# A fused mixer and expert kernel: the third down products moved to the down bank, one expert later

## The chip, the cores and the metric

One core of a Trainium2 chip runs the whole kernel in one launch. The metric is device time in microseconds; before the change the median of three runs is 716.4 us (715.74 to 717.3).

## The reference

256 tokens of 1024 channels pass through two hybrid layers (attention over selected keys, a compressed and windowed attention, a short convolution, a pooling mixer) and a norm, then through a second block: a state-space and attention mixer, a layer norm, and a mixture of 16 experts, all in float32. The change lies in the experts alone:

```python
weights = g_val[:, None] * e_val
expert_id = g_idx[:, None] * EXPERTS_PER_GROUP + e_idx
combine = jnp.sum(jax.nn.one_hot(expert_id, N_EXPERTS) * weights[..., None], axis=1)
for e in range(N_EXPERTS):
    act = jax.nn.silu(hf @ w_gate[e]) * (hf @ w_up[e])
    out = out + combine[:, e:e + 1] * (act @ w_down[e])
```

Two experts are chosen for a token, so an expert has 32 tokens on average, and the numbers are known only at run time. A layer norm of the residual and `out` ends the kernel.

## The kernel before, in words

**Blocks.** `experts` (L1941) walks over the 16 experts in four quarters of four; `e` is the expert, `j = e % 4` its place and `q = e // 4` its quarter. For a quarter, `gather_all` multiplies the normed tokens by one-hots (`picks`, on VectorE) and so brings the quarter's tokens into `xg`: 64 places for each expert, and 32 more. `gate_up` (L1730) computes gate and up for blocks of 32 tokens: the first block always, into the PSUM bank `gu`; the second under a branch for more than 32 tokens and the third under one for more than 64, into banks of the tag `s`. Where a block isn't computed, a one-column matmul (`none`, L1726) stands in for it. In this data the experts 0, 2, 4, 6, 8, 10 and 12 have more than 32 tokens, and 4 and 8 have more than 64.

**From gate and up to the output.** `activate` (L1765) reads `gu` on ScalarE and VectorE (L1773, L1774), applies SiLU and the product, and writes `sg`; it then does the same for the second and third block under branches. `turn` (L1791) transposes `sg` on TensorE and copies it to `aT` (two buffers); it is called as `mid`, between the sixth and the seventh of the eight weight tiles of the *next* expert's first block. `down` (L1806) multiplies `aT` by the down weights into the bank `dn`, for up to 64 tokens, and `take` (L1813) copies or adds `dn` into the rows `y[0]` of the expert. `third` (L1832) is the down product of the tokens 64 to 95, under a branch, with a `none` in its place otherwise, and `take_third` (L1841) adds it into `y2`, also under a branch. After every second expert `split_all` (L1859) multiplies the rows of two experts by their routing weights and splits them in a high and a low part (L1856 on ScalarE, L1857 on VectorE), and `scatter_all` (L1682) adds them to the output banks `acc` by matmuls with the turned one-hots `oT`. `spread` (L1628) makes `oT`: it turns the one-hots on TensorE into `dn` in two lots, and ScalarE copies each (L1637).

**Order.** The engines run their programs in the order written; `manual_schedule` keeps it. In the turn of expert `e` it is, for TensorE: the first block of `e` with `turn(e - 1)` inside, the other blocks, a scatter or a spread where due, `down(e - 1)`, `third(e - 1)`. For ScalarE and VectorE: the copy of `turn`, `activate(e)`, `take(e - 1)`, `take_third(e - 1)`, then splits, or the next quarter's `picks` (VectorE, `j == 2`) ahead of the splits. The spread of the first quarter is made in expert 0, that of the others in their third expert (`j == 2`). Expert 15 has an order of its own (L1973 to L1980).

**Weights.** Each expert has three loads of 2 MB, (gate, up) in two and down in one, which SyncE's queue fetches in a fixed order into ten ring buffers (`fill`, L275; the issue is L292). A load is issued when `give_back` (L302) has returned a buffer: those of gate and up after the expert's blocks, that of down after `third`.

A 32-column float32 matmul over 512 columns appears as two records, so the first block (16 matmuls) is 32 records, 24 of them ahead of the turn and 8 behind it.

Of the kernel before, what the change touches and what calls it, by code (L numbers as in the profile page):

```python
# [246 lines left out]
class Net:  # L247
# [1479 lines left out]

        self.nc.tensor.matmul(b[:, 0:1], self.zero, w.bitcast(BF16)[:, 1:2], start=True, stop=True)

    def gate_up(self, e, mid=None):  # L1730

        j, tc = e % 4, self.tc
        ws, rs = zip(*[self.load() for _ in range(2)])
        ws = [a.rearrange("p (k n) -> p k n", k=4) for a in ws]

        def w(k):
            return ws[k // 4][:, k % 4, :]

        def x(s):
            return lambda k: self.S["xg"][:, k, s:s + 32]  # L1740
        banks = self.gus = [self.gu]

        def before():
            if mid:
                mid()
            banks.extend(self.mbank("s") for _ in range(2))

        def none(i):
            for a in ws[2 - i:]:
                self.none(banks[i], a[:, 0, 0:1])  # L1750
        if e + 1 < N_EXP:
            self.count(e + 1)
        self.product32(banks[0], w, KT, x(64 * j), before)
        with tc.If(self.n[e] > 32) as more:
            self.product32(banks[1], w, KT, x(64 * j + 32))
            with tc.If(self.n[e] > 64) as much:
                self.product32(banks[2], w, KT, x(256 + 32 * j))
            with much.Else():
                none(2)
        with more.Else():  # L1760
            none(1)
            none(2)
        self.give_back(*rs)
# [67 lines left out]

    def third(self, e, aT, wd):  # L1832

        b = self.gu
        with self.tc.If(self.n[e] > 64) as more:
            self.product32(b, lambda k: wd[:, k, :], 4, lambda k: aT[:, k, 64:96])
        with more.Else():
            self.none(b, wd[:, 0, 0:1])
        return b
# [101 lines left out]
    def experts(self):  # L1941
        nc, m = self.nc, self.mw
        self.acc = [[self.ps.tile([P, HALF], F32, name=f"acc{t}{h}") for h in range(2)] for t in range(NT)]
        self.gu, self.dn = (self.ps.tile([P, HALF], F32, name=n) for n in ("gu", "dn"))
        self.clear(self.gu)
        self.clear(self.dn)
        for a in self.acc:
            for b in a:
                self.open(b)
        self.sg = m.tile([P, HALF], F32, name="sg")  # L1950
        nc.gpsimd.memset(self.sg, 0.0)
        S = self.S = {}
        self.wq = {}
        NQ = N_EXP // 4

        def gather_all():
            S["xg"] = m.tile([P, KT, 384], F32, name="xg")
            for k in range(KT):
                self.gather(self.oh, S["xg"], k)
                if k == KT - 1:  # L1960
                    self.wq[len(self.wq)] = self.weights(len(self.wq), self.oh)
        gather_all()
        self.residual()
        self.n, self.na = {}, {}
        self.count(0)
        aT = oT = None
        wd = lambda w: w.rearrange("p (k n) -> p k n", k=4)
        E = mybir.EngineType
        nq = naq = None
        for e in range(N_EXP):  # L1970
            q, j = divmod(e, 4)
            more, last = q + 1 < NQ, e == N_EXP - 1
            if last:  # L1973
                aT = self.turn(e - 1)
                self.scatter_all(oT[:, 0, :])
                w, r = self.load()
                self.down(e - 1, aT, wd(w))
                self.take(e - 1)
                self.split_all(slice(0, 64), self.wq[q][:, 1:2])
                self.gate_up(e)  # L1980
            else:
                def mid():
                    nonlocal aT
                    aT = self.turn(e - 1)
                self.gate_up(e, mid if e else None)
            if j == 0 and q:
                c = self.cnt[0:1, 16 + q:17 + q]
                nq = nc.values_load(c, engines=(E.PE,), min_val=0, max_val=T)
                naq = nc.values_load(c, engines=(E.Activation, E.DVE), min_val=0, max_val=T)
            if j == 1 and q:  # L1990
                self.scatter_all(oT[:, 1, :])
            if j == 2 and q:
                with self.tc.If(nq > 64) as much:
                    self.scatter_all(oT[:, 2, :])
                with much.Else():
                    for h in range(2):
                        for y in self.y[1:]:
                            self.nc.tensor.matmul(self.acc[1][h][:, 0:1], self.zero,
                                                  y.bitcast(BF16)[:, h * D + 1:h * D + 2], start=False, stop=False)
                oT = self.spread(self.oh)  # L2000
            if e == 0:
                oT = self.spread(self.oh)
            if j == 3 and more:
                self.scatter_all(oT[:, 0, :])
            if e and not last:
                w, r = self.load()
                self.down(e - 1, aT, wd(w))
            self.activate(e)
            if e and not last:
                self.take(e - 1)  # L2010
                b = self.third(e - 1, aT, wd(w))
                self.give_back(r)
                self.take_third(e - 1, b, self.na[e - 1])
            if j == 1 and q:
                with self.tc.If(naq > 64):
                    self.split_third(q - 1, self.y[1:])
            if j == 2:
                if more:
                    self.oh = self.picks(q + 1)
                self.split_all(slice(0, P), self.wq[q][:, 0:1])  # L2020
            if j == 0 and q:
                self.split_all(slice(0, P), self.wq[q - 1][:, 1:2])
            if j == 3 and more:
                gather_all()
        self.tc.mark_branch_hint_location("further", "LikelyTaken")
        for _ in range(WARM[3]):
            self.clear(self.dn)
        a0, aT = aT, self.turn(N_EXP - 1)
        i = self.free.pop()
        self.last = self.rings[i].tile([P, 4096], F32, name=f"wchunk{i}")  # L2030
        for i in range(2):
            self.row(4 + i, self.last[:, i * D:(i + 1) * D], eng=nc.sync)
        free = list(self.free)[:4]
        left = [(N_EXP - 2, a0, wd(w))]
        w, r = self.load()
        left.append((N_EXP - 1, aT, wd(w)))
        for _ in range(WARM[4]):
            self.clear(self.dn)
        self.down(N_EXP - 1, aT, wd(w))
        self.take(N_EXP - 1, True)  # L2040
        self.further(free, left, oT)
        self.scatter_all(oT[:, 1, :], last=True)
# [65 lines left out]
```

## Time and profile before

| | |
|---|---|
| median of three runs | 716.4 us |
| the profiled execution's own time | 718.6 us |
| its span, from first to last instruction | 716.8 us |
| TensorE matmul busy | 634.8 us (89%) |
| VectorE busy | 445.2 us (62%) |
| ScalarE busy | 315.1 us (44%) |
| mean granted TensorE clock | 0.947 |
| HBM traffic | 227 GB/s over the span |
| expert stage, first block of expert 0 to first block of expert 15 | 443.1 to 686.8 us |

The page gives busy time by engine, the span in 40 slices of 17.9 us with digits for tenths, and the costliest groups of instructions. The list of waits names who waited for whom; the instruction that released a wait is inferred, and where a wait has several conditions the last one seen is named. The timeline lists instructions in order of time with the idle time before them in brackets.

### The profile page before, as it was taken

How to read it: one execution, taken by the hardware profiler on the slowest of the kernel's cores; microseconds unless marked ns; L12 is line 12 of the kernel's file. 1: busy time of each engine (PE TensorE's matmuls, PEld its weight loads, DVE VectorE, ACT ScalarE, POOL GpSimd, SP SyncE). 2: the span in 40 equal slices, each digit the busy share in tenths (PEclk: the TensorE clock that was granted, in tenths of full speed). 3: DMA queues.
4: the chain of work that ended last, by engine and by line, in shares of the span. 5: the costliest groups of instructions: out<-in, count | busy, mean ns of one | idle time of the engine just before them, and what ended most of it. 6: DMA issues, size and time to landing. Idle time of an engine off the chain costs nothing. (4 is left out here: it accounts for less than half of the span.)

```text
span 716.8 us, 11754 instructions
## 1 busy us (share of the span) xinstructions
PE 634.8 (89%) x4487; PEld 444.0 (62%) x4487; DVE 445.2 (62%) x1050; ACT 315.1 (44%) x618; POOL 7.2 (1%) x29
## 2 busy tenths in 40 slices
PE   8999999899899999999999989789786978698772
PEld 4799888688897887888898665225221513253221
DVE  5798677878986796977788858243323332334235
ACT  5664555557455545435455424323323332324330
POOL 1000000000000000000000000000000000000001
PEclk9999999999999999999899989899898989999985
DMA  8946323244550045745033399999899959987211
GB/s 320 427 149 237 121 85 118 89 176 144 220 225 1 5 144 208 280 155 199 1 118 119 130 416 388 375 432 423 349 427 375 385 218 424 383 368 272 102 63 61
DMA packets 15917, 163.65 MB, mean 228 GB/s; under 512 B 1888, under 2 KB 2144, under 8 KB 6624
## 3 DMA queue, kind: packets, MB, share of 16 engines
q1 hardware_dynamic: 15552, 161.84, 56.8%
q8 instruction: 48, 0.79, 0.4%
q10 hardware_dynamic: 288, 0.79, 0.3%
q14 instruction: 29, 0.24, 0.1%
HBM read 161.57 MB, written 1.05 MB: 227 GB/s over the span
## 5 line engine op out<-in xcount | busy, mean ns | idle before, releaser
L318 ACT ACTIVATE whi<-wchunk 128x1024 fp32r<-128x1024 f32 (+2 forms) x103 | 107.4, 1042 | 94.1 <-PE pj L420 49.0
L319 DVE TENSOR_TENSOR wlo<-wchunk,whi 128x1024 fp32r<-128x1024 f32 (+2 forms) x103 | 123.2, 1198 | 20.1 <-ACT whi L318 19.8
L419 PE MATMUL pj<-xh,whi 128*128 128x256 f32 (+1 forms) x440 | 126.6, 288 | 0.0
L420 PE MATMUL pj<-xl,whi 128*128 128x256 f32 (+1 forms) x440 | 126.1, 287 | 0.0
L421 PE MATMUL pj<-xh,wlo 128*128 128x256 f32 (+1 forms) x440 | 125.1, 284 | 0.0
L1716 PE MATMUL gu<-wchunk,xg 128*32 128x512 f32 x512 | 75.7, 721 | 38.0 <-ACT y L1856 27.1
L419 PEld LDWEIGHTS pj<-xh,whi 128*128 128x128 f32 (+1 forms) x440 | 82.4, 187 | 3.2 <-issue 2.2
L420 PEld LDWEIGHTS pj<-xl,whi 128*128 128x128 f32 (+1 forms) x440 | 82.5, 188 | 2.8 <-issue 1.9
L421 PEld LDWEIGHTS pj<-xh,wlo 128*128 128x128 f32 (+1 forms) x440 | 82.6, 188 | 1.8 <-issue 1.6
L1774 DVE TENSOR_TENSOR tg<-tg,gu 64x256 f32<-64x256 f32 x32 | 13.2, 413 | 91.2 <-ACT tg L1773 91.2
L1716 PEld LDWEIGHTS gu<-wchunk,xg 128*32 128x32 f32 x512 | 17.6, 124 | 70.3 <-issue 34.4
L420 PE MATMUL pj<-wlo,xh 128*128 128x512 f32 (+2 forms) x112 | 40.8, 364 | 1.6 <-DVE wlo L319 1.6
L419 PE MATMUL pj<-whi,mh 128*128 128x512 f32 x96 | 39.2, 412 | 2.6 <-ACT mh L510 2.1
L420 PE MATMUL pj<-wlo,mh 128*128 128x512 f32 x96 | 38.5, 403 | 2.5 <-DVE wlo L319 2.4
L421 PE MATMUL pj<-whi,xl 128*128 128x512 f32 (+2 forms) x112 | 40.5, 362 | 0.0
L419 PE MATMUL pj<-whi,xh 128*128 128x512 f32 (+2 forms) x112 | 39.5, 358 | 0.5 <-ACT whi L318 0.4
L421 PE MATMUL pj<-whi,ml 128*128 128x512 f32 x96 | 38.0, 404 | 0.0
L553 ACT ACTIVATE prob<-bank,smst 128x128 f32<-128x128 f32 (+1 forms) x64 | 26.1, 418 | 18.4 <-DVE smst L551 18.4
L1798 ACT ACTIVATE aT<-mbs 128x384 f32<-128x384 f32 x16 | 7.8, 490 | 58.9 <-PE mbs L1796 58.9
L1716 PE MATMUL mbs<-wchunk,xg 128*32 128x512 f32 x288 | 32.2, 592 | 0.0
L1679 PE MATMUL acc<-y,oT 128*128 128x512 f32 x80 | 24.7, 453 | 4.5 <-PEq L1869 2.9
L1723 PE MATMUL dn<-wchunk,aT 128*64 128x512 f32 x112 | 25.6, 598 | 0.0
(415 smaller groups left out, 1052.6 us busy)
## 6 DMA issues: line engine op xcount, KB each, us to landing
wchunk<-wstream SPq DMA_DIRECT2D x67, 2048.0 KB, 9.9
wchunk<-wstream SPq DMA_DIRECT2D x12, 512.0 KB, 10.5
wchunk<-wstream SPq DMA_DIRECT2D x2, 1536.0 KB, 9.3
wchunk<-wstream SPq DMA_DIRECT2D x2, 1024.0 KB, 8.4
wchunk<-wstream SPq DMA_DIRECT2D x4, 436.0 KB, 5.6
wchunk<-wstream SPq DMA_DIRECT2D x1, 1744.0 KB, 6.8
wchunk<-xt SPq DMA_DIRECT2D x4, 256.0 KB, 5.5
X<-x SPq DMA_DIRECT2D x4, 256.0 KB, 5.8
```

Of the source, the lines that this page charges most:

```text
L318: nc.scalar.activation(hi, w, AF.Copy)
L319: nc.vector.tensor_sub(lo, w, hi.bitcast(F32))
L419: mm(out, ah, bh, start=start, stop=False)
L420: mm(out, ah, bl, start=False, stop=False)
L421: mm(out, al, bh, start=False, stop=stop)
L553: nc.scalar.activation(p[:, e, j, :N], S[e][:, j, :], AF.Exp, bias=nm[:, e, j:j + 1], accum_out=sm[:, e, j:j + 1])
L1679: self.nc.tensor.matmul(self.acc[t][h], oT[r, t * P:(t + 1) * P], y[1 + i], start=False, stop=last and i == 1, **at)
L1716: self.nc.tensor.matmul(out[r:r + 32, :], lhs(k), w(k)[:, HALF * i:HALF * i + HALF], start=(k < 2), stop=(k >= n - 2), tile_position=(0, r))
L1723: self.nc.tensor.matmul(out[64 * i:64 * i + 64, :], lhs(k), w(k)[:, HALF * i:HALF * i + HALF], start=(k == 0), stop=(k == n - 1), tile_pos ...
L1774: V.tensor_add(tg[0:64, 0, s], tg[0:64, 0, s], b[0:64, s])
L1798: nc.scalar.activation(aT.rearrange("p a n -> p (a n)"), ps[:, 0:4 * n], AF.Copy)
```

## The change

The third down product goes to `dn` instead of `gu`, and it is called (with `give_back` and `take_third`) by the next expert but one's `gate_up`, behind the first block: in the turn of expert `e + 1` for expert `e - 1`. For that the transposed activations of two experts are kept (`a0`, `aT`). In expert 15 it is called ahead of the scatter. The first quarter's spread is made with expert 2, as the other quarters' are with their third expert.

```diff
-    def gate_up(self, e, mid=None):
+    def gate_up(self, e, mid=None, end=None):
...
         self.product32(banks[0], w, KT, x(64 * j), before)
+        if end:
+            end()
         with tc.If(self.n[e] > 32) as more:
...
     def third(self, e, aT, wd):
 
-        b = self.gu
+        b = self.dn
...
-        aT = oT = None
+        a0 = aT = oT = third = None
...
             if last:
-                aT = self.turn(e - 1)
+                a0, aT = aT, self.turn(e - 1)
+                third()
                 self.scatter_all(oT[:, 0, :])
...
                 def mid():
-                    nonlocal aT
-                    aT = self.turn(e - 1)
-                self.gate_up(e, mid if e else None)
+                    nonlocal a0, aT
+                    a0, aT = aT, self.turn(e - 1)
+                self.gate_up(e, mid if e else None, third if e > 1 else None)
...
-                oT = self.spread(self.oh)
-            if e == 0:
+            if j == 2:
                 oT = self.spread(self.oh)
...
                 self.take(e - 1)
-                b = self.third(e - 1, aT, wd(w))
-                self.give_back(r)
-                self.take_third(e - 1, b, self.na[e - 1])
+
+                def third(e=e - 1, w=w, r=r):
+                    b = self.third(e, a0, wd(w))
+                    self.give_back(r)
+                    self.take_third(e, b, self.na[e])
```

## Rows read from the trace of the kernel before

**Rows 1.** The page's 40 slices of the span: TensorE's granted clock, DMA's share.

```profile
PEclk9999999999999999999899989899898989999985
DMA  8946323244550045745033399999899959987211
```

**Rows 2.** List of TensorE's waits, 443 to 690 us: total, times, longest.

```profile
PE gu L1716 <- ACT y L1856: 27.1, 6, 5.4
```

**Rows 3.** TensorE timeline: first blocks of experts 1, 2, 3, 5, 6, 7, 9, 10, 11, 13, 14.

```profile
454.08 5.35 PE L1716 MATMUL gu<-wchunk,xg 128*32 128x512 f32 x24 [2.19 <-DVE tg L1774]
...
466.50 2.78 PE L1716 MATMUL gu<-wchunk,xg 128*32 128x512 f32 x24 [1.54 <-ACTq L1843]
...
479.15 4.29 PE L1716 MATMUL gu<-wchunk,xg 128*32 128x512 f32 x24 [2.86 <-ACT y L1856]
...
516.09 5.32 PE L1716 MATMUL gu<-wchunk,xg 128*32 128x512 f32 x24 [5.35 <-ACT y L1856]
...
532.72 2.78 PE L1716 MATMUL gu<-wchunk,xg 128*32 128x512 f32 x24 [2.30 <-issue]
...
550.15 5.35 PE L1716 MATMUL gu<-wchunk,xg 128*32 128x512 f32 x24 [5.38 <-ACT y L1856]
...
588.00 5.20 PE L1716 MATMUL gu<-wchunk,xg 128*32 128x512 f32 x24 [5.32 <-ACT y L1856]
...
604.52 2.78 PE L1716 MATMUL gu<-wchunk,xg 128*32 128x512 f32 x24 [2.30 <-issue]
...
623.75 4.40 PE L1716 MATMUL gu<-wchunk,xg 128*32 128x512 f32 x24 [5.38 <-ACT y L1856]
...
655.05 4.11 PE L1716 MATMUL gu<-wchunk,xg 128*32 128x512 f32 x24 [2.86 <-ACT y L1856]
...
667.98 2.78 PE L1716 MATMUL gu<-wchunk,xg 128*32 128x512 f32 x24 [1.55 <-ACTq L1843]
```

**Rows 4.** Windows: stretch, length, engines' busy, granted clock, DMA share, GB/s last.

```profile
573.98:594.68 20.70, 15.38 (x121) 4.19 (x113) 7.15 (x12) 6.49 (x12) 0.00 (x0) 0.84 0.62 251
594.68:608.78 14.10, 11.80 (x83) 4.49 (x87) 5.13 (x9) 4.67 (x9) 0.00 (x0) 1.00 1.02 433
```

**Rows 5.** VectorE timeline ahead of expert 5: activation's end, take, splits.

```profile
513.79 0.68 DVE L1777 TENSOR_TENSOR sg<-tg 32x512 f32<-32x512 f32 x1 [0.69 <-ACT tg L1776]
514.54 1.39 DVE L1804 TENSOR_TENSOR y<-tg,dn 32x512 f32<-32x512 f32 x2
516.08 1.42 DVE L1857 SCALAR_TENSOR_TENSOR y<-y,wq,y 128x512 fp32r<-128x512 f32 x2
```

**Rows 6.** VectorE timeline of expert 0: its last read of the first block.

```profile
453.62 0.41 DVE L1774 TENSOR_TENSOR tg<-tg,gu 64x256 f32<-64x256 f32 x1 [0.45 <-ACT tg L1773]
```

**Rows 7.** Weight loads: the issue for expert 5, and landing times, 440 to 660 us.

```profile
464.99 0.33 SPq L292 DMA_DIRECT2D wchunk<-wstream  x1
...
DMA to landing us min/median/max: 7.4/12.2/19.1
```

**Rows 8.** TensorE timeline: the scatter in expert 15.

```profile
681.02 0.50 PE L1679 MATMUL acc<-y,oT 128*128 128x512 f32 x1 [1.35 <-ACT y L1856]
681.81 3.35 PE L1679 MATMUL acc<-y,oT 128*128 128x512 f32 x7 [0.29 <-DVE y L1857]
```

**Rows 9.** TensorE timeline: a scatter; the spreads in experts 0 and 6, down after it.

```profile
672.26 2.10 PE L1679 MATMUL acc<-y,oT 128*128 128x512 f32 x8
...
450.14 0.63 PE L1636 MATMUL dn<-cstm,oh 128*128 128x128 f32 x4
...
540.51 0.64 PE L1636 MATMUL dn<-cstm,oh 128*128 128x128 f32 x4
...
542.74 1.92 PE L1716 MATMUL dn<-wchunk,aT 128*32 128x512 f32 x16 [0.47 <-ACT oT L1637]
```

**Rows 10.** VectorE timeline ahead of expert 7: activation's end, splits.

```profile
547.39 0.68 DVE L1777 TENSOR_TENSOR sg<-tg 32x512 f32<-32x512 f32 x1 [0.70 <-ACTq L1781]
...
551.22 1.41 DVE L1857 SCALAR_TENSOR_TENSOR y<-y,wq,y 128x512 fp32r<-128x512 f32 x2
```

## The prediction

> **What bounds the kernel now.** I read the page's slices first: the end of the span (from about 443 us) is the expert stage, where the digits of TensorE's clock dip to 8 again and again, while DMA stands at eight to nine tenths in most slices [rows 1]. Two suspects, then: the weight stream, or TensorE's waits. The list of TensorE's waits names one place: the first matmul of `gate_up` on the bank `gu` (L1716), 27.1 us behind ScalarE's L1856 alone [rows 2]. The TensorE timeline shows all the places, one row per expert [rows 3]: eleven experts begin their first block after an idle time, 37.0 us together, and in seven of them the 24 records before the turn take 4.1 to 5.35 us where the other four take 2.78; the excess is 34.0 - 7 x 2.78 = 14.6 us. The reader is to see a clock effect in it: over expert 9's stretch from 573.98 the granted clock is 0.84, over expert 10's, whose block takes 2.78, it is 1.00 [rows 4]; TensorE came back from the long waits at 1.2 GHz.
>
> What is waited for? For expert 5, TensorE goes idle at 516.09 - 5.35 = 510.74. VectorE finishes the activation of expert 4 at 514.47, then the two adds of `take(3)` at 515.93, and `gu` starts 0.16 us later [rows 5]. So `gu` is not waiting for its weights, nor for its own reader, but for `take_third(3)`, which stands behind `activate(4)` and `take(3)` on ScalarE and VectorE and nominally reads `gu`. The first boundary proves the other half: no third product exists yet, and `gu` of expert 1 starts at 454.08, right after the first part of `activate(0)` has read the bank (454.03), with more of that activation still to come [rows 6].
>
> The stream is not the bound. The first weights of expert 5 were issued at 464.99; no landing took over 19.1 us; they are used at 516.09, over 30 us later [rows 3, 7]. At the end too: the stream falls to two tenths in the slice from 663 us, while the last expert's block begins after 685 [rows 1, 8].
>
> **The change, part by part.** *Third product into `dn`, after the next but one expert's first block.* `gu` then has one reader, the first part of `activate`, over long before TensorE comes back; the first block starts as soon as the down product is issued. All of the 37.0 us idle and the 14.6 us excess go [rows 3]. In their place come three waits within the block: the turn waits for the end of `activate`, the third product (or its one-column stand-in) for `take` to have read `dn`, and the scatter two steps later for the splits of `y`. Behind them on TensorE stand the second block, scatter and down product. Without waits, the way from the first block's start to the end of the scatter is 672.26 + 2.10 - 667.98 = 6.4 us [rows 3, 9].
>
> At experts 5 and 9, counted from where TensorE now goes idle: activation ends at +3.7, `take` at +5.2, the first low split at 516.08 + 0.71 - 510.74 = +6.05 [rows 5]. The block (2.78, turn, last part: 4.3) fits between, and the scatter, whose second matmul needs that low split, ends at 6.05 + 7/8 x 2.10 = 7.9. So 1.6 us of new waits each.
>
> At experts 3, 7 and 11 the next quarter's one-hots stand ahead of the splits on VectorE. Idle begins at 550.15 - 5.38 = 544.77; activation ends at +3.3, the first low split at 551.22 + 0.71 - 544.77 = +7.15 [rows 3, 10]; scatter ends at 9.0: 2.6 us of new waits each. At expert 13 the split is through in time. At experts 2, 6, 10 and 14 `activate` is over already, so nothing comes back. The two real third products (experts 4 and 8, issued now at 6 and 10) keep their matmuls; their `take_third` lies beside the second block. Experts 4, 8 and 12 follow a gather and have no idle to lose: nothing.
>
> *Spread of the first quarter moved from expert 0 to 2.* From expert 0 it takes 454.08 - 2.19 - 450.14 = 1.75 us of TensorE [rows 3, 9], and lets `activate(0)` start with the block instead of behind the spread's copies; so the turn of expert 0 finds its activation done. At expert 2 it costs what it costs at expert 6: 542.74 - 540.51 = 2.2 us [rows 9], and expert 2's activation then ends as late as expert 6's (that is the +3.3 used above).
>
> *Rings.* The down weights' buffer comes back in the next expert's block instead of at this expert's end; SyncE's queue issues the same loads in the same order, one in three about an expert later against the TensorE program. The lead of 30 us hides it. If that cover were gone, each microsecond a load is late would stand on TensorE. Branches and the moved stand-in: the stand-in matmul and its branch are there before too; I price them at 0, bounded by 0.2 us an expert above and by nothing gained below. At expert 15 the added `third()` waits for a `take` for which the scatter's splits wait anyway: 0.
>
> **Sum.** 37.0 + 14.6 + 1.75 = 53.3 us goes; back come 2.2 (spread), 3 x 2.6 and 2 x 1.6: 13.2. That leaves 40.1 us.
>
> One cost is not shown in the place where it would arise: the clock after several short waits. A wait of 1.54 or even 2.30 us left the block at 2.78, one of 2.86 made it 4.3 [rows 3]. But the end of the stage shows the very pattern that experts 3, 7 and 11 get: a turn, a scatter's first matmul, a short idle; there seven scatter matmuls took 3.35 us instead of 1.84 [rows 8]. Bounds: 0, and the worst excess, 5.35 - 2.78 = 2.57, at all five experts (12.9). I take 1.5 us at three, as the nearest row: 4.5. Net 40.1 - 4.5 = 35.6 us.
>
> The Trainium skill, "TensorE: Matmul & The Clock Gate", section "A second HAM failure mode: psum-queue depth-cycling", speaks against this change: frequent small idles between groups of matmuls can make the clock swing between its two levels, so the work between them is paid for at the lower one. The trace agrees for the pattern of [rows 8] and not for the lone 2.30 us wait; by the rule in full the forecast would be the second rival's.
>
> The profiled execution took 718.6 us (span 716.8), 2.2 over the median of 716.4; I subtract from the median: **716.4 - 35.6 = 680.8 us**. From the profiled one it would be 683.0.
>
> **Rivals.**
>
> *`gu` is still held by the whole activation.* The branches inside `activate` could make the release come at their end. Against it: the start at 454.08 [rows 6]. For it: only one such boundary exists. Then the first block starts at +3.8 for experts 5 and 9 (scatter at 3.8 + 6.4 = 10.2, not 7.9) and +3.4 for 3, 7, 11 (9.8, not 9.0), about 2.7 late at expert 1 and 0.8 at 13: 4.6 + 2.4 + 3.5 = 10.5, and two more blocks at the low clock, 3.0: about 694.
>
> *The clock swings at every one of the five experts with new waits.* At 2.57 each, 12.9 instead of 4.5: 680.8 + 8.4 = 689. For it [rows 8]; against it the 2.30 us waits that cost nothing [rows 3].
>
> *The weight stream becomes the bound.* An expert's 6.29 MB take 14.5 us at the 433 GB/s of a stretch with full queues [rows 4]; TensorE now takes (667.98 - 454.08) / 13 = 16.45 us an expert, and would take about 13.7. So the stream falls behind by 0.8 us an expert, some 10 us in all, inside the lead. Short of that lead, most of the gain goes and the time is 700 to 716.
>
> *Slower than before:* the same place, TensorE's first matmul on late weights, with the buffer that is held an expert longer halving the lead to about 16 us. It decides where the stream stays below 6.29 / (16.45 + 16 / 13) = 355 GB/s; at 340 it gives 13 x (18.5 - 16.45) - 16 = 10.6 us more, 727. Low rates exist, 251 GB/s, but at a DMA share of 0.62, so with queues out of work [rows 4], which makes it unlikely.
>
> **Numbers.** Forecast 0.62; clock swing 0.17; whole activation 0.10; stream takes most of the gain 0.06; slower by the stream 0.05. The range reaches from no clock loss (716.4 - 40.1 = 676.3, and 1.5 for the branches and roundings) to the first rival and 2 over: 675 to 696. All cases but the last end faster; of the stream's, half could come within 0.2%, about what a measurement can tell from no change: faster 0.92, same 0.03, slower 0.05.
>
> **What would show it.** Right: the list of TensorE's waits loses `gu` behind L1856; the first block follows the down product at once in experts 1, 2, 5, 6, 7, 9, 10, 11, 13, 14 and takes 2.78; new waits stand at the turn (L1796) and at the scatter (L1679) of experts 3, 5, 7, 9 and 11, 1 to 2 us each; `dn` one-hot turns run once per quarter, the first behind expert 2. Wrong: a wait of more than 1 us at `gu`'s first matmul (first rival); `gu` waiting for a DMA (the stream); scatter and down product at 1.2 GHz in experts 5 and 9 (clock); a wait at the stand-in in `dn` that reaches far beyond the end of `take`.

## The result, and the profile after

The changed kernel takes 688.5 us, median of four runs (686.5 to 690.7), against 716.4: a ratio of 0.961 with a 95% interval of 0.958 to 0.964. The gain is 27.9 us, 35.6 were forecast; the time lies inside the range, 7.7 us above the forecast. The profiled execution took 686.5 us with a span of 684.7.

The page first: TensorE's busy time, the digits of its clock and of DMA, and the group of the first block's matmuls.

```profile
PE 624.8 (91%) x4487; PEld 444.9 (65%) x4487; DVE 445.0 (65%) x1050; ACT 315.3 (46%) x618; POOL 7.2 (1%) x29
...
PEclk9999999999999999999989998999999999999985
DMA  8946323225363024655303339999999999999411
...
L1716 PE MATMUL gu<-wchunk,xg 128*32 128x512 f32 x512 | 61.0, 596 | 0.9 <-DVE wq L1652 0.9
```

From the slice of 428 us to the last two, the clock digits stay at 9 where they dipped to 8 four times [rows 1] (a short dip can hide in a 9), and the stream stands at nine tenths nearly to its end. The last line is the one to read: the idle time before the first blocks is 0.9 us in all, and that is expert 0's; ahead of the eleven blocks of [rows 3], where it was 37.0, none is left. Their matmuls take 596 ns each, and every first block of the experts 1 to 14 has its 24 records in 2.76 to 2.78 us, as the fast ones had before. The expert stage, from the first block of expert 0 to that of expert 15, fell from 243.8 us to 213.3.

What stands in place of the waits on `gu` is shown by the list of TensorE's waits in the expert stage (total, times, longest), which answers to [rows 2]. In the changed kernel `turn` is L1798, the splits on ScalarE are L1858, those on VectorE L1859.

```profile
PE mbs L1798 <- DVEq L1783: 3.4, 4, 1.0
PE mbs L1798 <- DVE sg L1779: 2.8, 2, 1.4
PE acc L1679 <- issue: 2.8, 2, 2.4
...
PE mbs L1798 <- DVEq L1781: 2.6, 2, 1.8
PE mbs L1728 <- ACTq L1845: 2.6, 5, 0.6
PE dn L1728 <- ACT y L1858: 2.4, 4, 1.3
...
PE mbs L1728 <- PE dn L1728: 1.7, 5, 0.4
```

The turns wait for the activation (L1779, L1783), as expected. In the experts 3 to 11 the scatter does not wait for the splits at all; the stand-in matmuls (L1728) wait instead. (The rows hold three waits of other experts: 0.28 us at the turn in expert 1's block, both waits behind L1781, at the turns of the experts 14 and 15, and the 1.3 at `dn`, which stands in expert 15 where the scatter waited 1.35 before [rows 8].) TensorE's timeline of expert 5 shows the new waits in order, and answers to the row of 516.09 in [rows 3]:

```profile
502.39 2.76 PE L1716 MATMUL gu<-wchunk,xg 128*32 128x512 f32 x24
506.57 0.52 PE L1798 MATMUL mbs<-cstm,sg 96*128 96x96 f32 x4 [1.42 <-DVE sg L1779]
507.02 1.07 PE L1716 MATMUL gu<-wchunk,xg 128*32 128x512 f32 x8
508.02 0.18 PE L1728 MATMUL dn<-wchunk,zero 128*128 128x1 bf16 x1
508.53 0.16 PE L1728 MATMUL mbs<-wchunk,zero 128*128 128x1 bf16 x1 [0.33 <-PE dn L1728]
509.22 0.19 PE L1728 MATMUL mbs<-wchunk,zero 128*128 128x1 bf16 x2 [0.52 <-ACTq L1845]
509.27 3.61 PE L1679 MATMUL acc<-y,oT 128*128 128x512 f32 x8
```

Waits of 1.42, 0.33 and 0.52 us, and then a scatter of 3.61 us, which at the upper clock takes 2.1 [rows 9]. The granted clock (the number after POOL's column; the others as in [rows 4]) is 0.53 over this scatter, and 1.00 over expert 9's, which takes 2.09:

```profile
509.27:512.88 3.61, 3.61 (x12) 2.37 (x13) 1.83 (x5) 1.60 (x4) 0.00 (x0) 0.53 1.02 424
570.52:572.53 2.01, 2.01 (x10) 1.40 (x9) 1.28 (x4) 1.46 (x4) 0.00 (x0) 1.00 1.01 432
```

The 0.52 us belongs to the stand-in for the third block. ScalarE's timeline says why:

```profile
507.27 1.38 ACT L1858 ACTIVATE y<-y,wq 128x512 fp32r<-128x512 f32 x2 [0.95 <-DVE y L1806]
508.67 0.49 ACT L1800 ACTIVATE aT<-mbs 128x384 f32<-128x384 f32 x1
```

The copy of the turn (L1800) stands behind the two splits; it ends at 509.16, and only then is the turn's bank free again for the third block's stand-in, which runs at 509.22.

One more stretch is new, in expert 13:

```profile
626.45 0.71 PE L1679 MATMUL acc<-y,oT 128*128 128x512 f32 x2
629.57 2.72 PE L1679 MATMUL acc<-y,oT 128*128 128x512 f32 x6 [2.40 <-issue]
```

A hole of 2.40 us in the middle of a scatter, with no engine that ends it; the six matmuls behind it run at a granted clock of 0.50.

### The profile page after: what moved, and what is told of

It is laid out like the page before. It is cut to its first block, busy times and chain, and to the rows that moved or that the text cites. A ratio compares the mean times of both kernels' runs of the same rounds, so it can differ in the third digit from the quotient of the medians.

```text
span 684.7 us, 11761 instructions
## 1 busy us (share of the span) xinstructions
PE 624.8 (91%) x4487; PEld 444.9 (65%) x4487; DVE 445.0 (65%) x1050; ACT 315.3 (46%) x618; POOL 7.2 (1%) x29
## 5 line engine op out<-in xcount | busy, mean ns | idle before, releaser
L1716 PE MATMUL gu<-wchunk,xg 128*32 128x512 f32 x512 | 61.0, 596 | 0.9 <-DVE wq L1652 0.9
L1679 PE MATMUL acc<-y,oT 128*128 128x512 f32 x80 | 32.2, 558 | 6.1 <-issue 2.8
L1716 PEld LDWEIGHTS gu<-wchunk,xg 128*32 128x32 f32 x512 | 14.6, 109 | 30.3 <-issue 25.2
L1679 PEld LDWEIGHTS acc<-y,oT 128*128 128x128 f32 x80 | 20.7, 271 | 13.2 <-issue 3.3
L1806 DVE TENSOR_TENSOR y<-tg,dn 32x512 f32<-32x512 f32 x22 | 14.9, 680 | 21.4 <-ACT tg L1829 12.0
```

The costliest lines, as they stand in the source:

```text
L1679: self.nc.tensor.matmul(self.acc[t][h], oT[r, t * P:(t + 1) * P], y[1 + i], start=False, stop=last and i == 1, **at)
L1716: self.nc.tensor.matmul(out[r:r + 32, :], lhs(k), w(k)[:, HALF * i:HALF * i + HALF], start=(k < 2), stop=(k >= n - 2), tile_position=(0, r))
L1806: self.nc.vector.tensor_add(dst, self.t3[r, :], b[r, :])
```

## The experiments

### The changed kernel once more

No edit.

> The changed kernel as it is, once more. Theory (the wait on the bank gu is gone, short waits and 3.4 us stretches at 1.2 GHz are what is left): 686 to 691 us, the scatters of experts 3, 5, 7 and 11 at 3.6 us again. The 2.4 us hole in the scatter of expert 13, which no engine releases: if it is a late fetch of instructions, it may lie elsewhere or be absent, and its presence moves the time by 2 to 3 us; if it belongs to the change, it stands in the same place with the same length.

688.1 us, median of six (684.9 to 690.4); ratio 0.960 (0.956 to 0.963). TensorE's timeline in experts 5, 9 and 13:

```profile
510.82 2.09 PE L1679 MATMUL acc<-y,oT 128*128 128x512 f32 x8
...
570.44 3.56 PE L1679 MATMUL acc<-y,oT 128*128 128x512 f32 x8
...
631.68 2.39 PE L1679 MATMUL acc<-y,oT 128*128 128x512 f32 x6 [2.68 <-issue]
```

The expectation on the scatters missed in part: expert 5's is fast here and expert 9's slow, the reverse of the first profile, though the waits ahead of expert 5's are the same (1.43, 0.33, 0.52). Those of the experts 3, 7 and 11 are slow again (3.84, 3.61 and 3.08 us). So at two of the five experts the slow stretch comes and goes from run to run. The runs spread over 5.5 us, but so did those of the kernel before beside them (6.0). The hole stays in its place.

### The third products alone

```diff
-            if j == 2:
+            if e == 0 or (j == 2 and q):
                 oT = self.spread(self.oh)
```

> The third products moved as in the change, the first spread left with expert 0. Theory: expert 1 keeps its 2.2 us idle and slow first block and the spread before it (6.3 us), expert 2 saves its spread (2.1) and expert 3 finds its splits done early (3.7): within 2 us of the changed kernel, 687 to 691. Rival (the spread's move is worth the 4 us that it frees at expert 1): 692 to 693.

688.0 us, ratio 0.960 (0.956 to 0.963): the same as the whole change. Expert 1's first block, and expert 3's scatter:

```profile
452.53 5.35 PE L1716 MATMUL gu<-wchunk,xg 128*32 128x512 f32 x24 [2.18 <-DVE tg L1776]
...
477.32 2.37 PE L1679 MATMUL acc<-y,oT 128*128 128x512 f32 x8
```

Expert 1 keeps its wait and slow block as in [rows 3], and expert 3, whose splits are now early, scatters with no wait before it and nearly at full pace. What expert 1 loses, experts 2 and 3 get back.

### The spread alone

```diff
-                oT = self.spread(self.oh)
-            if e == 0:
+            if j == 2:
                 oT = self.spread(self.oh)
```

(on the kernel before)

> The first spread moved to expert 2, the third products left in gu at the end of each expert. Theory: expert 1 gains 6.3 us, expert 2 pays 2.1 for the spread and expert 3 starts after a 5.4 us wait instead of 2.9 with a slower block (3.6): 715 to 717, no change that counts. Rival: 712.

716.2 us, ratio 0.9998 (0.998 to 1.002): no difference, as the theory had it. Expert 3 pays for expert 1:

```profile
474.72 4.48 PE L1716 MATMUL gu<-wchunk,xg 128*32 128x512 f32 x24 [5.38 <-ACT y L1856]
```

It was 4.29 after 2.86 [rows 3]. As far as the runs can tell, the whole gain of the change is the third products'.

### The bank alone, at the old place

```diff
     def third(self, e, aT, wd):
-        b = self.gu
+        b = self.dn
```

(on the kernel before)

> The third product in the bank dn, but at its old place at the end of the expert, ahead of the next first block. Theory (the place matters, since the product now waits for take there): 713 to 716, the waits of 2.9 and 5.4 us now stand at the stand-in matmul in dn instead of at gu. Rival (it is the bank alone: gu is free, so the first block starts early): 688 to 695.

730.7 us, ratio 1.020 (1.016 to 1.023): 14 us slower. The direction of the rival is refuted, and the size of the theory's too. TensorE's waits, then its timeline at experts 5 and 7:

```profile
PE dn L1728 <- ACT y L1856: 30.3, 7, 5.5
PE dn L1728 <- DVEq L1843: 8.1, 5, 1.6
PE gu L1716 <- issue: 4.1, 7, 0.7
PE dn L1716 <- DVE y L1823: 3.3, 2, 1.6
```

```profile
518.51 0.16 PE L1728 MATMUL dn<-wchunk,zero 128*128 128x1 bf16 x1 [5.43 <-ACT y L1856]
519.25 5.29 PE L1716 MATMUL gu<-wchunk,xg 128*32 128x512 f32 x24 [0.58 <-issue]
...
567.36 0.16 PE L1728 MATMUL dn<-wchunk,zero 128*128 128x1 bf16 x1 [1.63 <-DVEq L1843]
```

The wait of 5.4 us is whole again, now at the stand-in in `dn`. New are waits of 1.6 us ahead of the gathers (the last row), where `gu` had been free: in `dn` the stand-in waits for `take` in every expert. And the first block behind the stand-in starts 0.6 us late, with no engine that releases it; that the branches around the stand-in are worked off only when the wait is over is argued, not tested. The bank alone is a loss, so the gain needs the new place. Whether it needs the new bank too is open: the new place with the old bank was not run.

### The short waits filled

```diff
         ps = self.mbank("s")
+        for _ in range(4 if e in (2, 4, 6, 8, 10) else 0):
+            self.clear(ps)
...
             self.none(b, wd[:, 0, 0:1])
+            for _ in range(2 if e in (1, 3, 5, 7, 9) else 0):
+                self.clear(b)
```

(`clear` is a bf16 matmul of zeros over 512 columns, into a bank that is overwritten next)

> The changed kernel with one-pass bf16 matmuls of zeros in the short waits: four ahead of the turn in experts 3, 5, 7, 9 and 11, two behind the stand-in of the third product there. Theory (the short waits bring the clock down, and the scatter behind them pays): the scatters of experts 3, 5, 7 and 11 take 2.1 us instead of 3.6, 682 to 685 us. Rival (the clock falls for the kind of work, or at its own times): scatters at 3.6 us, 688 to 691.

678.6 us, median of five (677.5 to 678.8), ratio 0.946 (0.944 to 0.949): by the ratios 9.5 us under the changed kernel, more than the theory asked. TensorE's timeline of expert 5, and the window from 525 to 640 us (columns as in [rows 4]), here and in the changed kernel:

```profile
503.77 1.04 PE L599 MATMUL mbs<-zero 128*128 128x512 bf16 x4
505.17 0.55 PE L1800 MATMUL mbs<-cstm,sg 96*128 96x96 f32 x4 [0.36 <-DVE sg L1779]
...
507.90 0.19 PE L1728 MATMUL mbs<-wchunk,zero 128*128 128x1 bf16 x2 [0.62 <-ACTq L1849]
507.95 2.09 PE L1679 MATMUL acc<-y,oT 128*128 128x512 f32 x8
```

```profile
525.00:640.00 115.00, 107.10 (x762) 46.92 (x762) 49.60 (x95) 46.79 (x91) 0.00 (x0) 1.00 0.99 418
...
525.00:640.00 115.00, 103.31 (x724) 46.03 (x716) 46.39 (x88) 43.42 (x83) 0.00 (x0) 0.96 1.00 417
```

The scatter begins as long after its first block's start as before (6.9 us in both), so what the scatter depends on has not come sooner; it takes 2.09 instead of 3.61. Scatters of experts 3, 7 and 11 take 2.4, with the granted clock at 1.00 there too, so the 0.3 us are not the clock's. The granted clock is 1.00 over the window; the changed kernel's is 0.96 over the same window of its own. The hole in expert 13 is gone as well, and that makes a part of the 9.5 us, as the next experiment shows. The five runs spread over 1.2 us.

### The hole

```diff
         self.clear(self.gu)
-        self.clear(self.dn)
+        for _ in range(31):
+            self.clear(self.dn)
```

> The changed kernel with 30 matmuls of zeros ahead of the expert stage, as many as the filled kernel had in its waits by expert 13, so that the program of TensorE from there on lies where it lay in the filled kernel; the waits stay as in the changed kernel. They cost about 6.5 us. Theory (the 2.4 us hole in the scatter of expert 13 is a fetch of instructions, tied to the place in the program): the hole is gone, or lies elsewhere, and the scatters of experts 3, 5, 7 and 11 are still slow; 690 to 693. Rival (the hole comes from the waits or the clock): the hole of 2.2 to 2.7 us is in the same scatter; 693 to 697.

690.6 us, ratio 0.964 (0.961 to 0.968). The 30 matmuls put the start of the stage off more than expected, from 441.39 to 449.73 us, 8.3; without them it is 682.3, some 6 under the changed kernel. In the profiles the stage, from the first block of expert 0 to that of expert 15, takes 209.8 us; in the two of the changed kernel it takes 213.3 and 215.9, in the filled one 205.5. So, its own cost aside, the shift alone brings 3.5 to 6 us, and of the filled kernel's 9.5 some 4 are the fill's. Expert 5's scatter, and expert 13's:

```profile
517.70 3.50 PE L1679 MATMUL acc<-y,oT 128*128 128x512 f32 x8
...
634.99 2.10 PE L1679 MATMUL acc<-y,oT 128*128 128x512 f32 x8
```

The slow scatter is still there, the hole is not: expert 13 now takes 10.0 us from block to block, against 13.75. So the hole does not come with the waits. The shift moved the stage in time as well, but the other profiles speak for the place in TensorE's program and not for the time. With the down product ahead of the scatter (the next kernel) it stands in the down product, again behind the first few matmuls after expert 13's stand-ins:

```profile
634.93 5.35 PE L1723 MATMUL dn<-wchunk,aT 128*64 128x512 f32 x15 [2.41 <-issue]
```

There it begins 191 us after the start of the stage, in the changed kernel 186. That a fetch of instructions fills it is argued, not shown: in the changed kernel's hole (626.9 to 629.6 us) the instruction queue moved one packet,

```profile
q8 instruction: 1, 0.02, 2.3%
```

but such a packet passes at other times too, with no hole beside it.

### Down product ahead of the scatter

```diff
-            if j == 1 and q:
-                self.scatter_all(oT[:, 1, :])
...
-            if j == 3 and more:
-                self.scatter_all(oT[:, 0, :])
             if e and not last:
                 w, r = self.load()
                 self.down(e - 1, aT, wd(w))
+            if j == 1 and q:
+                self.scatter_all(oT[:, 1, :])
+            if j == 3 and more:
+                self.scatter_all(oT[:, 0, :])
```

> The changed kernel with the down product ahead of the scatter in the second and fourth expert of a quarter. Theory (what stops TensorE there is the stand-in matmuls, whose bank waits for the copy of the turn behind the splits on ScalarE, not the scatter's own wait): 686 to 690, the slow stretch moves into the down product. Rival (the scatter's wait for the splits is the cost): 681 to 685.

693.3 us, ratio 0.968 (0.965 to 0.971): 3 us above the theory's range, and further still from the rival's. Expert 7 on TensorE, and VectorE's splits there:

```profile
537.65 0.19 PE L1728 MATMUL mbs<-wchunk,zero 128*128 128x1 bf16 x2 [0.53 <-ACTq L1845]
539.01 5.35 PE L1723 MATMUL dn<-wchunk,aT 128*64 128x512 f32 x16 [1.17 <-DVEq L1845]
```

```profile
537.44 1.41 DVE L1859 SCALAR_TENSOR_TENSOR y<-y,wq,y 128x512 fp32r<-128x512 f32 x2
```

The stand-ins wait as before, which the theory had. What it lacked: the down product writes `dn`, so it waits until VectorE has passed `take_third` (L1845), which stands behind the splits that end at 538.85. The scatter had covered that. And the slow stretch now lies in a longer product.

### Splits behind the turn's copy

The same with `split_all` called by the next `gate_up`'s `end`, behind `third()`:

```diff
+                def end():
+                    nonlocal split
+                    third()
+                    if split:
+                        split()
+                        split = None
...
-                self.split_all(slice(0, P), self.wq[q][:, 0:1])
+                split = lambda w=self.wq[q]: self.split_all(slice(0, P), w[:, 0:1])
```

(and so for `self.wq[q - 1]`)

> As the last, and the splits of two experts' rows are issued behind the next turn's copy instead of ahead of it. Theory: the stand-ins no longer wait, the splits lie beside the down product, 2 to 2.5 us less at each of experts 3, 5, 7, 9 and 11: 677 to 681. Rival (the splits then delay the activation on VectorE and give it back): 686 to 690.

683.0 us, ratio 0.952 (0.949 to 0.955): better by 5, not by the 7 to 11 of the theory. Expert 7:

```profile
532.79 0.25 PE L1728 MATMUL mbs<-wchunk,zero 128*128 128x1 bf16 x3 [0.34 <-PE dn L1728]
533.52 6.59 PE L1723 MATMUL dn<-wchunk,aT 128*64 128x512 f32 x16 [0.48 <-DVEq L1845]
```

The stand-ins no longer wait for the copy; the waits at the turn remain, and with them, in this profile, one slow stretch among the five experts, at expert 7, that falls on the down product (6.59 us; 3.65 at the upper clock). The hole is there too, 2.6 us in expert 13's down product.

And with the fill ahead of the turn:

```diff
         ps = self.mbank("s")
+        for _ in range(4 if e in (2, 4, 6, 8, 10) else 0):
+            self.clear(ps)
```

> As the last, with the four matmuls of zeros ahead of the turn. Theory: if the wait at the turn alone still brings the clock down, up to 1.5 us at each of five experts less than the last; if the clock stays up without them, no difference beyond 1 us.

678.0 us, ratio 0.947 (0.944 to 0.949): 5 us less than without it, and level with the filled kernel. The slow stretch at expert 7 is gone, which is 2.9 us between the two profiles, and of the hole 1.3 us are left, now ahead of expert 13's other stand-ins:

```profile
619.68 0.24 PE L1728 MATMUL mbs<-wchunk,zero 128*128 128x1 bf16 x3 [1.31 <-issue]
```

From expert 13's block to expert 14's that is another 3.0 us, so here too the fill's part and the hole's stand side by side. What the later splits save beside the fill can't be told from nothing.

### The fill at the end too

On the filled kernel:

```diff
-WARM = (18, 12, 3, 4, 2)
+WARM = (18, 12, 3, 10, 2)
...
-        for _ in range(4 if e in (2, 4, 6, 8, 10) else 0):
+        for _ in range(4 if e in (2, 4, 6, 8, 10, 14) else 0):
             self.clear(ps)
...
-            for _ in range(2 if e in (1, 3, 5, 7, 9) else 0):
+            for _ in range(2 if e in (1, 3, 5, 7, 9) else 6 if e == 13 else 0):
                 self.clear(b)
```

> The filled kernel with the same matmuls of zeros in the waits of expert 15 too (four ahead of the turn, six behind its stand-in, six more ahead of the last turn). Theory (the clock falls there for the same reason: the scatter of expert 15 takes 4.1 us instead of 2.1): 2 us less at that scatter and little behind it, 675 to 677. Rival: the end is set by the chain of the last rows, which the fill does not touch: 678 to 679.

677.2 us, median of six (676.9 to 679.2), ratio 0.947 (0.944 to 0.949). Expert 15 in the filled kernel, and with this edit:

```profile
639.79 4.14 PE L1679 MATMUL acc<-y,oT 128*128 128x512 f32 x8
...
638.18 1.02 PE L599 MATMUL mbs<-zero 128*128 128x512 bf16 x4 [0.83 <-DVEq L1781]
...
640.00 1.46 PE L599 MATMUL dn<-zero 128*128 128x512 bf16 x6
641.11 2.19 PE L1679 MATMUL acc<-y,oT 128*128 128x512 f32 x8
```

The scatter takes 2.19 us instead of 4.14. But the four matmuls ahead of the turn had to wait 0.83 us themselves, as long as the turn did without them, so they stand behind the wait and put the turn off. The medians are 1.4 us apart, and the ratios' intervals overlap. The filled kernels beat both the kernel before and the changed one; which of the three is best is open.

## Why the prediction was right, and where it was short

*The wait.* Right. `gu` was held by `take_third` behind `take`; with the third product gone, the first block follows the down product at once and at full pace. The rival that the whole activation holds `gu` falls: expert 5's block starts at 502.39, and its turn still waits for the activation four microseconds later.

*The new waits.* Right in sum by luck, wrong in place. 3 x 2.6 and 2 x 1.6 is 11.0 us (the 1.6 should be 1.5 by the prediction's own rows: 7.9 - 6.4). The list of waits has 3.4 + 2.8 at the turns and 1.1 (2.4 less expert 15's 1.3) + 2.6 + 1.7 at the stand-ins, 11.6, of which 0.28 is expert 1's. But each of the five experts has 2.2 to 2.4: those priced at 2.6 got less, those priced at 1.6 more. The step that failed is "Branches and the moved stand-in: ... I price them at 0", with a bound of 0.2 us an expert: the stand-ins have 5.4 us of waits at the five experts, about 1.1 each. A stand-in is a matmul that writes a bank, so it waits like one (0.42 to 0.64 us for the turn's copy). Between two stand-ins stand another 0.23 to 0.45 us (0.33 at expert 5) that read as the branch's cost behind a wait, which was not tested by itself. The scatter's wait for the splits, put at 1 to 2 us, is covered by that.

*The clock.* The mechanism was right, the term mis-sized: 4.5 us were priced, at three experts. The first profile has slow scatters at four, 3.56 + 3.61 + 3.72 + 3.62 - 4 x 2.1 = 6.1 us; the second has four too, with expert 9's in place of expert 5's. The filled kernel and the shifted one settle the cause together: with matmuls of zeros in the same waits no scatter of the five experts is at the lower clock, with the same number of them ahead of the stage four still are. The Trainium skill's rule in "TensorE: Matmul & The Clock Gate", "A second HAM failure mode: psum-queue depth-cycling", that small idles between groups of matmuls make the clock swing, fits these four scatters (3.56 to 3.72 us) better than the row of the 2.30 us wait that was set against it. The second rival's time, 689, is nearer to the measured 688.5 than the forecast is, but that is in part luck: it asked for 12.9 us of clock where 6.1 are found, and the hole, which it did not have, brings it there.

*The hole.* Not in the prediction: 2.4 us and a slow rest of the scatter, 5.83 instead of 2.1 us in all, so 3.7. What fills it stays open.

*Together.* In the profiles the stage gained 30.5 us. From the forecast's 35.6 go 0.6 of waits, 1.6 of clock and 3.7 of hole: 29.7, so 0.8 are not accounted for. The rest of the profiles' 32.1 us is the stage's start, 1.7 us earlier in this run. The medians differ by 27.9 only: the profiled run of the kernel before was 2.2 us above its median, that of the changed kernel 2.0 below. What moves the time of a run by that much is not shown; the slow stretches that come and go may be part of it.

*The spread.* Predicted in pieces and never added up. Its pieces at expert 1 are 1.75 + 2.19 + 2.57 = 6.5, and what it brings to experts 2 and 3 is 2.2 + 2.6 + 1.5 = 6.3. Two runs show that sum: nothing.

*The stream.* Right: no wait for weights shows in TensorE's list of the changed kernel. But the DMA share is 0.99 in the filled kernel, and with the later splits and the fill one down product already waits 0.5 us for its weights, so little is left before the stream decides.

## What to carry to other kernels

A wait moves with the work that stands behind it, and another bank alone does not take it away: put the dependent work where the engine has other work ahead of it, and then ask of each stand-in and branch behind it which buffer it writes and whose copy frees that buffer. When a long wait has been broken into short ones, look at the granted clock of the work behind them; if it dips, cheap matmuls of zeros in the waits can be worth as much as making the waits shorter (some 4 us here), if they need nothing that the wait is for. Such matmuls also shift the program, so a shift alone has to be run beside them; and a hole that no engine ends is to be tried with a shifted program before it is explained by a dependency.

## What was not expected of the hardware

The same three waits (1.42, 0.33 and 0.52 us, ahead of expert 5's scatter) left the scatter at 3.61 us in one run and at 2.09 in the next: the clock's answer to short waits is not fixed by them. Matmuls of zeros kept the clock up: with them the granted clock stayed at 1.00 over 115 us in which it was 0.96 without. And a hole of 2.2 to 2.7 us in expert 13's stretch was in every profile of the changed kernel and of its variants (five) as long as the program ahead of it had its length; with 40 more instructions (the deferred splits with fill) 1.3 us were left, with 60 (the filled kernel and the shifted one) nothing.
